# Fixing the order of TensorE's products and transposes in a mixture-of-experts stage

## The chip, the cores and the metric

One core of a Trainium2 chip runs the whole program. The metric is the device time of one launch in microseconds (us); several launches are timed and the median is told. One more launch is profiled, and its trace is what the rows below come from.

## What is computed

Two transformer layers over 256 tokens of width 1024, in float32. Layer 0 has stick-breaking attention and a dense SwiGLU. Layer 1 has softmax attention and a mixture of 8 experts, two of them per token. Only the experts matter here:

```python
def swiglu(h, w1, w3, w2):
    hid = silu(h @ w1) * (h @ w3)
    return hid @ w2
# w1, w3: 1024 x 3584, w2: 3584 x 1024, for each of 8 experts
y = sum(swiglu(t, e_w1[e], e_w3[e], e_w2[e]) * gate[:, e])
```

The weights of the experts are 8 x 3 x 3584 x 1024 floats, 352 MB, and each is read once.

## The kernel before, in words

**Products.** A float32 product is made of three faster ones (`mm3`, lines 175 to 179): each operand is split into a high part (`wh`) and a low part (`wl`), and high x high, high x low and low x high are added up in one PSUM bank. ScalarE (ACT in the rows) makes `wh` by a copy (line 154), VectorE (DVE) makes `wl` by a subtraction (line 155), which needs `wh`. Both work on 128x1024 pieces, and there are four buffers for each of `wh` and `wl`, so that a fifth piece can be split only when TensorE has done the products of the first.

**Loads.** SyncE (SP) loads the weights in pieces of 1 MB (two 128x1024 pieces each) into a ring of `raw` buffers, in the order in which they are used; a load is issued as soon as its buffer has been split.

**An expert** (lines 942 to 987) is seven chunks of 512 hidden columns. One chunk is:

- 24 products with its part of `w1` into one bank (four pieces; here called a1 to a4), then 24 with `w3` into another (b1 to b4). The stationary operand, the expert's tokens (`eh`, `el`), lies in `oh_t`.
- `gate_mul` (lines 585 to 593): ACT computes Silu of the first bank (line 587), DVE multiplies by the second (line 588) into `nat`.
- `hid_t` (lines 595 to 601), called one chunk later, between the `w1` and the `w3` products of the next chunk: four transposes on TensorE (PE, line 599) turn `nat`, into the bank that held the `w1` products. Then `split_out` (lines 181 to 183) splits the result into `hts`, two tiles in `ol_t`: ACT first (line 182), then DVE (line 183). `hts` exists once, so that this split has to wait for the last product that reads the chunk before it.
- `down` (lines 603 to 606), called one chunk later too, after `gate_mul`: 24 products of `hts` with four pieces of `w2` (d1 to d4), which add up over the expert's seven chunks in banks 0 and 1.

So the source's order on TensorE is: a1 to a4 of a chunk, the transposes of the chunk before, b1 to b4, d1 to d4 of the chunk before. At the end of an expert the tokens of the next are turned (`turn_x`, lines 871 to 878), and after its last `down` the sums leave through `yr` (`store_y`, lines 857 to 861: ACT line 859, DVE line 860). In the last expert four additions of rows stand on DVE as well (`add_rows`, lines 845 to 850), and the products of the last two chunks wait for them through `after=added` in `gate_mul`.

**What sets the order.** The source gives the order of the statements, but a planner (`schedule_with_timeline_sim=True`, line 1129) chooses each engine's real order: it plays the program through with its own idea of durations and lets an engine take, at each moment, the first instruction in source order that is ready. That order is then fixed, and each engine works through it strictly, waiting where something is not there yet. `behind((a, b))` (lines 106 to 113) forces `a` to come after `b` on their engine, without a semaphore. In the loop over the experts the kernel before uses it for `turn_x`, for `gate_mul` with `after` and in `stream`, and not for the products or for `hid_t`.

Of the kernel before, what the change touches and what calls it, by code (L numbers as in the profile page):

```python
# [17 lines left out]
P = 128  # L18
# [3 lines left out]
NC = D // P  # L22
# [5 lines left out]
FC = 512  # L28
# [17 lines left out]
def block_kernel(ctx: ExitStack, tc: tile.TileContext, x, w_qkv, w_o, mixer_norm, ffn_norm,  # L46
                 rel_bias, w1, w3, w2, router, e_w1, e_w3, e_w2, final_norm, onehot, out):
    nc = tc.nc
# [9 lines left out]
    bank = [psp.tile([P, FC], F32, name=f"bank{i}") for i in range(8)]  # L58
# [20 lines left out]
    ecs = [(f, min(FC, DFE - f)) for f in range(0, DFE, FC)]  # L79
# [26 lines left out]
    def behind(*pairs):  # L106

        for a, b in pairs:
            if b is not None:
                tc.add_manual_dep(a.ins, b.ins.name,  # L110
                                  mybir.DependencyInfo(mybir.DependencyClass.NoSync,
                                                       mybir.DependencyReason.DATA),
                                  reason="issue order")
# [24 lines left out]
    def stream(n, g=None, hold=(None, None), free=2):  # L138


        got = taken = 0
        while got < n:
            load_ahead()
            t = loaded[n_used[0]]
            _, nk, fn = jobs[n_used[0]]
            n_used[0] += 1
            k = min(nk, HALF // fn)
            for c0 in range(0, nk, k):
                wh = split.tile([P, HALF], F32R, name="wh")
                wl = split.tile([P, HALF], F32R, name="wl")  # L150
                m = k * fn
                src = t[:, c0 * fn:c0 * fn + m]
                if g is None:
                    i0 = nc.scalar.activation(wh[:, :m], src, AF.Copy)  # L154
                    i1 = nc.vector.tensor_sub(wl[:, :m], src, wh[:, :m].bitcast(F32))  # L155
                    if taken >= free:
                        behind((i0, hold[0]), (i1, hold[1]))
                else:
                    for c in range(k):
                        cs = slice(c * fn, (c + 1) * fn)  # L160
                        gc = gcol[:, g, got + c0 + c:got + c0 + c + 1]
                        i0 = nc.scalar.activation(wh[:, cs], src[:, cs], AF.Copy, scale=gc)  # L162
                        i1 = nc.vector.scalar_tensor_tensor(  # L163
                            wl[:, cs], src[:, cs], gc, wh[:, cs].bitcast(F32), op0=ALU.mult,
                            op1=ALU.subtract)
                        if taken >= free:
                            behind((i0, hold[0]), (i1, hold[1]))
                recent[0] = i0
                taken += 1
                for c in range(k):  # L170
                    yield wh[:, c * fn:(c + 1) * fn], wl[:, c * fn:(c + 1) * fn]
            got += nk
        assert got == n

    def mm3(ps, s, m, start, stop):
        i0 = nc.tensor.matmul(ps, s[0], m[0], start=start, stop=False)  # L176
        nc.tensor.matmul(ps, s[0], m[1], start=False, stop=False)  # L177
        i1 = nc.tensor.matmul(ps, s[1], m[0], start=False, stop=stop)  # L178
        return i0, i1

    def split_out(src, h, l):
        return (nc.scalar.activation(h, src, AF.Copy),
                nc.vector.tensor_sub(l, src, h.bitcast(F32)))  # L183
# [30 lines left out]
    ident = const.tile([P, P], F32, name="ident")  # L214
# [377 lines left out]
                                           op1=ALU.mult)  # L592
        return t

    def hid_t(t, n, ps, a, c, apart=True):
        k = n // P
        tv = t[:, :n].rearrange("p (f j) -> p j f" if apart else "p (j f) -> p j f", j=k)
        for j in range(k):
            nc.tensor.transpose(ps[:, j * P:(j + 1) * P], tv[:, j], ident)
        split_out(ps[:, :n], a[:, :n], c[:, :n])  # L600
        return [(a[:, j * P:(j + 1) * P], c[:, j * P:(j + 1) * P]) for j in range(k)]

    def down(ps, hT, j, w, start, stop):
        for half in range(2):
            mm3(ps[half], hT[j], tuple(a[:, half * FC:(half + 1) * FC] for a in w),
                start and j == 0, stop and j == len(hT) - 1)

    def dense_ffn(pool, hold, then):
        y = [[bank[0], bank[1]], [bank[2], bank[7]]]
# [172 lines left out]
    eh, el = (sp[0][:, i * D:(i + 1) * D].rearrange("p (c t) -> p c t", t=P) for i in range(2))  # L782
    hts = [sp[1][:, i * FC:(i + 1) * FC] for i in range(2)]
# [6 lines left out]
    tv = mp.tile([P, 2, NB], F32, name="tv")  # L790
# [80 lines left out]
    def turn_x(t, banks, later):  # L871

        for i in range(2):
            for c in range(4):
                cc = 4 * i + c
                behind((nc.tensor.transpose(bank[banks[i]][:, c * P:(c + 1) * P],
                                            t[:, cc * P:(cc + 1) * P], ident), later))
            take(i, banks[i])

    def gather(banks, later):  # L880


        def part(b, i, later):
            ps = bank[banks[i]]
            for c in range(4):
                cc = 4 * i + c
                i0 = nc.tensor.matmul(ps[:, c * P:(c + 1) * P], hn[b][:, cc * P:(cc + 1) * P],
                                      pe[:, b].bitcast(F32), start=b == 0 and c == 0,
                                      stop=b == NB - 1 and c == 3, skip_group_check=True)
                behind((i0, later))  # L890

        mark(0, 0)
        part(0, 0, later)
        later = numbers(1)
        part(0, 1, later)
        held[1] = mark(0, 1)
        for i in range(2):
            part(1, i, later)
            take(i, banks[i])
# [14 lines left out]
    y = [bank[0], bank[1]]  # L914
# [18 lines left out]
                i1 = nc.vector.tensor_add(ht[b][:, hs], ht[b][:, hs], ps)  # L933
        return i0, i1

    pend, done, added = None, None, None
    gather((3, 4), raws[2])
    k = 0
    most_v = None
# [2 lines left out]
    for e in range(NE):  # L942
        for i, (f0, n) in enumerate(ecs):
            b1, b3 = (5, 6) if k % 2 == 0 else (3, 4)
            k += 1
            for bk in (b1, b3):
                if bk == b3:
                    held[:] = None, None
                for c, w in enumerate(stream(NC, hold=held)):
                    _, last = mm3(bank[bk], (eh[:, c], el[:, c]), w, c == 0, c == NC - 1)  # L950
                if pend is not None and bk == b1:
                    hT = hid_t(pend[1], FC, bank[pend[2]], *hts)
            if i == len(ecs) - 1 and e + 1 < NE:
                turn_x(xr, (2, 7), last)
            t = gate_mul(ep.tile([P, FC], F32, name="nat"), bank[b1], bank[b3], n, after=added)
            if pend is not None:
                for j, w in enumerate(stream(4)):
                    down(y, hT, j, w, pend[0] == 0, pend[0] == len(ecs) - 1)
            pend = (i, t, b1)
            if i == 0:  # L960
                if e:
                    store_y(e - 1)
                else:
                    gates()
                    send()

                    cps = bank[2]
                    for b in range(NB):
                        nc.tensor.matmul(cps[:, :NE], ones, sel[:, b], start=b == 0,
                                         stop=b == NB - 1)  # L970
                    most = mp.tile([P, 1], F32, name="most")
                    nc.vector.tensor_reduce(most, cps[:, :NE], axis=mybir.AxisListType.X,
                                            op=ALU.max)
                    most_i = mp.tile([P, 1], mybir.dt.int32, name="most_i")
                    nc.vector.tensor_copy(most_i, most)
                    nc.vector.tensor_scalar(pos2, slot, -float(P), None, op0=ALU.add)
            if i == 1 and e + 1 < NE:
                xr = load_x(e + 1)
            if e == NE - 1:
                if i == 0:  # L980
                    for b in range(NB):
                        mark(e, b)
                    done = slots(e)
                elif i == 2:
                    came = [fetch(b) for b in range(NB)]
                elif i in (4, 5):
                    added = add_rows(i - 4, came[i - 4])
    hT = hid_t(pend[1], FC, bank[pend[2]], *(sp[0][:, i * FC:(i + 1) * FC] for i in range(2)))

    row = ep.tile([P, FC], F32, name="nat")  # L990
# [78 lines left out]
    for half in range(2):  # L1069
# [3 lines left out]
        i0, i1 = scatter(done, (half,), hts if half else ys)  # L1073
# [5 lines left out]
    for b in range(NB):  # L1079
# [3 lines left out]
        i1 = nc.vector.scalar_tensor_tensor(ms, ss[:, b, 1:2], 1.0 / D, ms, op0=ALU.mult,  # L1083
                                            op1=ALU.add)
# [49 lines left out]
```

## Time and profile before

| | |
|---|---|
| median of 3 launches | 1440.25 us (1438.56 to 1440.41) |
| profiled launch, its own time | 1438.46 us |
| its span, first to last instruction | 1436.8 us |
| TensorE | busy 1417.6 us (99%), 7285 matmuls and transposes |
| VectorE | busy 1170.2 us (81%) |
| ScalarE | busy 1010.3 us (70%) |
| mean granted TensorE clock | 0.996 of 2.4 GHz |
| DMA | 442.11 MB, mean 308 GB/s |

In the profile an instruction stands with the line that made it. A row of the timeline merges equal instructions in a row (x4 are four of them), and its first two numbers are the start of the first and the time from there to the end of the last. In brackets stands how long the engine was idle before, and whose result ended that. PEld is the load of the stationary operand of a product; it runs ahead of the products, so that a wait often shows there and not at PE. The ends of PE's instructions are modelled, so its starts are what is read here. The span's first 430 us or so are layer 0 and the attention of layer 1; the experts run from about 453 us to 1425 us.

### The profile page before, as it was taken

How to read it: one execution, taken by the hardware profiler on the slowest of the kernel's cores; microseconds unless marked ns; L12 is line 12 of the kernel's file. 1: busy time of each engine (PE TensorE's matmuls, PEld its weight loads, DVE VectorE, ACT ScalarE, POOL GpSimd, SP SyncE). 2: the span in 40 equal slices, each digit the busy share in tenths (PEclk: the TensorE clock that was granted, in tenths of full speed). 3: DMA queues.
4: the chain of work that ended last, by engine and by line, in shares of the span. 5: the costliest groups of instructions: out<-in, count | busy, mean ns of one | idle time of the engine just before them, and what ended most of it. 6: DMA issues, size and time to landing. Idle time of an engine off the chain costs nothing. (4 is left out here: it accounts for less than half of the span.)

```text
span 1436.8 us, 19637 instructions
## 1 busy us (share of the span) xinstructions
PE 1417.6 (99%) x7285; PEld 1176.7 (82%) x7285; DVE 1170.2 (81%) x1384; ACT 1010.3 (70%) x1282; POOL 45.3 (3%) x71
## 2 busy tenths in 40 slices
PE   9999999999999999999999999999999999999997
PEld 7877999988877888888888888878878887887775
DVE  6656766667667999999999988888888888898887
ACT  6656655546655778878878777777777777777765
POOL 1000000000001000000000000000000000000200
PEclk9999999999999999999999999999999999999998
DMA  9633865556566999999999999999999999999850
GB/s 353 236 117 108 303 196 186 186 173 228 180 246 218 402 401 388 385 373 373 388 392 362 391 362 373 366 381 368 354 389 372 357 380 380 358 374 369 320 189 32
DMA packets 172153, 442.11 MB, mean 308 GB/s; under 512 B 7299, under 2 KB 9395, under 8 KB 157972
## 3 DMA queue, kind: packets, MB, share of 16 engines
q1 hardware_dynamic: 166852, 422.61, 80.6%
q0 software_dynamic: 5136, 18.18, 3.5%
q8 instruction: 59, 0.97, 0.3%
q14 instruction: 42, 0.34, 0.1%
q10 hardware_dynamic: 64, 0.02, 0.0%
HBM read 430.00 MB, written 11.03 MB: 307 GB/s over the span
## 5 line engine op out<-in xcount | busy, mean ns | idle before, releaser
L155 DVE TENSOR_TENSOR wl<-raw,wh 128x1024 fp32r<-128x1024 f32 x710 | 834.4, 1220 | 112.9 <-ACT wh L154 106.0
L154 ACT ACTIVATE wh<-raw 128x1024 fp32r<-128x1024 f32 x710 | 725.6, 1057 | 133.9 <-PE bank L178 97.7
L177 PE MATMUL bank<-wl,oh_t 128*128 128x512 f32 x968 | 382.9, 396 | 2.9 <-DVE wl L155 2.0
L176 PE MATMUL bank<-wh,oh_t 128*128 128x512 f32 x968 | 375.5, 393 | 2.1 <-ACT wh L154 1.6
L178 PE MATMUL bank<-wh,oh_t 128*128 128x512 f32 x904 | 353.5, 391 | 0.1
L177 PEld LDWEIGHTS bank<-wl,oh_t 128*128 128x128 f32 x968 | 181.9, 188 | 60.0 <-DVE wl L155 18.9
L176 PEld LDWEIGHTS bank<-wh,oh_t 128*128 128x128 f32 x968 | 182.2, 188 | 41.4 <-ACT wh L154 1.8
L178 PEld LDWEIGHTS bank<-wh,oh_t 128*128 128x128 f32 x904 | 170.2, 188 | 34.1 <-DVE oh_t L183 0.8
L178 PE MATMUL bank<-wh,ol_t 128*128 128x512 f32 x504 | 194.6, 392 | 0.0
L162 ACT ACTIVATE wh<-raw,gcol 128x512 fp32r<-128x512 f32 (+1 forms) x192 | 123.8, 698 | 87.4 <-PE bank L318 56.3
L163 DVE SCALAR_TENSOR_TENSOR wl<-raw,gcol,wh 128x512 fp32r<-128x512 f32 (+1 forms) x192 | 131.1, 725 | 65.8 <-ACT wh L162 65.3
L177 PE MATMUL bank<-wl,ol_t 128*128 128x512 f32 x440 | 174.7, 397 | 0.4 <-DVE wl L155 0.4
L318 PE MATMUL bank<-x_h,wh 128*128 128x256 f32 x512 | 143.8, 282 | 0.0
L318 PE MATMUL bank<-x_h,wl 128*128 128x256 f32 x512 | 142.9, 280 | 0.0
L318 PE MATMUL bank<-x_l,wh 128*128 128x256 f32 x512 | 142.7, 279 | 0.0
L176 PE MATMUL bank<-wh,ol_t 128*128 128x512 f32 x440 | 137.1, 393 | 0.0
L178 PEld LDWEIGHTS bank<-wh,ol_t 128*128 128x128 f32 x504 | 94.4, 188 | 19.9 <-issue 1.1
L318 PEld LDWEIGHTS bank<-x_h,wh 128*128 128x128 f32 x512 | 95.9, 188 | 1.9 <-issue 1.1
L177 PEld LDWEIGHTS bank<-wl,ol_t 128*128 128x128 f32 x440 | 83.0, 189 | 16.4 <-DVE wl L155 0.6
L318 PEld LDWEIGHTS bank<-x_h,wl 128*128 128x128 f32 x512 | 96.1, 188 | 0.0
L318 PEld LDWEIGHTS bank<-x_l,wh 128*128 128x128 f32 x512 | 95.9, 187 | 0.2
L176 PEld LDWEIGHTS bank<-wh,ol_t 128*128 128x128 f32 x440 | 81.6, 188 | 16.8
(218 smaller groups left out, 1106.1 us busy)
## 6 DMA issues: line engine op xcount, KB each, us to landing
raw<-in_e_w_dram SPq DMA_DIRECT2D x335, 1024.0 KB, 7.3
raw<-in_w_dram SPq DMA_DIRECT2D x33, 1024.0 KB, 5.1
raw<-in_w_qkv_dram SPq DMA_DIRECT2D x22, 1024.0 KB, 5.7
raw<-in_w_o_dram SPq DMA_DIRECT2D x8, 1024.0 KB, 7.5
xs_d<-hn POOLq DMA_DIRECT2D x1, 4096.0 KB, 16.0
xr<-xs_d POOLq DMA_DIRECT2D x7, 512.0 KB, 7.5
ys_d<-yr POOLq DMA_DIRECT2D x7, 512.0 KB, 7.8
raw<-in_w_qkv_dram SPq DMA_DIRECT2D x4, 512.0 KB, 6.8
```

The source lines that it names most:

```text
L154: i0 = nc.scalar.activation(wh[:, :m], src, AF.Copy)
L155: i1 = nc.vector.tensor_sub(wl[:, :m], src, wh[:, :m].bitcast(F32))
L162: i0 = nc.scalar.activation(wh[:, cs], src[:, cs], AF.Copy, scale=gc)
L163: i1 = nc.vector.scalar_tensor_tensor(wl[:, cs], src[:, cs], gc, wh[:, cs].bitcast(F32), op0=ALU.mult, op1=ALU.subtract)
L176: i0 = nc.tensor.matmul(ps, s[0], m[0], start=start, stop=False)
L177: nc.tensor.matmul(ps, s[0], m[1], start=False, stop=False)
L178: i1 = nc.tensor.matmul(ps, s[1], m[0], start=False, stop=stop)
L318: nc.tensor.matmul(to, w[a][:, ms], z[:, :, c], start=c + i + m % 2 == 0, stop=c == NC - 1 and m % 2 == 1 and i == 2, skip_group_check=True)
```

## The change

`hid_t` and `down` get an argument `after`, and the loop over the experts carries `last`, the last product issued. Every group of three products of `w1` is put behind the last product of `down` before it, those of `w3` behind the last of `w1`, those of `down` behind the last of `w3`; the four transposes are chained behind the last product of `w1` and behind each other. Nothing else is changed: no instruction is added or removed, and no order is written for ScalarE, VectorE or the loads.

```diff
-    def hid_t(t, n, ps, a, c, apart=True):
+    def hid_t(t, n, ps, a, c, apart=True, after=None):
         k = n // P
         tv = t[:, :n].rearrange("p (f j) -> p j f" if apart else "p (j f) -> p j f", j=k)
         for j in range(k):
-            nc.tensor.transpose(ps[:, j * P:(j + 1) * P], tv[:, j], ident)
+            i0 = nc.tensor.transpose(ps[:, j * P:(j + 1) * P], tv[:, j], ident)
+            if after is not None:
+                behind((i0, after))
+                after = i0
         split_out(ps[:, :n], a[:, :n], c[:, :n])
         return [(a[:, j * P:(j + 1) * P], c[:, j * P:(j + 1) * P]) for j in range(k)]

-    def down(ps, hT, j, w, start, stop):
+    def down(ps, hT, j, w, start, stop, after=None):
         for half in range(2):
-            mm3(ps[half], hT[j], tuple(a[:, half * FC:(half + 1) * FC] for a in w),
-                start and j == 0, stop and j == len(hT) - 1)
+            i0, i1 = mm3(ps[half], hT[j], tuple(a[:, half * FC:(half + 1) * FC] for a in w),
+                         start and j == 0, stop and j == len(hT) - 1)
+            behind((i0, after))
+        return i1
...
-    pend, done, added = None, None, None
+    pend, done, added, last = None, None, None, None
...
                 for c, w in enumerate(stream(NC, hold=held)):
-                    _, last = mm3(bank[bk], (eh[:, c], el[:, c]), w, c == 0, c == NC - 1)
+                    i0, i1 = mm3(bank[bk], (eh[:, c], el[:, c]), w, c == 0, c == NC - 1)
+                    behind((i0, last))
+                last = i1
                 if pend is not None and bk == b1:
-                    hT = hid_t(pend[1], FC, bank[pend[2]], *hts)
+                    hT = hid_t(pend[1], FC, bank[pend[2]], *hts, after=last)
             if i == len(ecs) - 1 and e + 1 < NE:
                 turn_x(xr, (2, 7), last)
             t = gate_mul(ep.tile([P, FC], F32, name="nat"), bank[b1], bank[b3], n, after=added)
             if pend is not None:
                 for j, w in enumerate(stream(4)):
-                    down(y, hT, j, w, pend[0] == 0, pend[0] == len(ecs) - 1)
+                    i1 = down(y, hT, j, w, pend[0] == 0, pend[0] == len(ecs) - 1, last)
+                last = i1
```

## Rows read from the trace of the kernel before

**Rows 1.** Stretches by windows: length, busy time of each engine, clock, DMA share, GB/s.
```profile
480.18:598.96 118.78, 118.78 (x542) 98.81 (x541) 110.20 (x102) 96.01 (x102) 1.69 (x3) 1.00 1.03 393
598.96:717.72 118.76, 118.76 (x541) 98.80 (x540) 110.19 (x102) 95.99 (x102) 1.07 (x2) 1.00 1.01 380
835.90:957.50 121.60, 121.42 (x541) 97.80 (x540) 107.64 (x102) 92.01 (x102) 1.07 (x2) 1.00 1.01 372
...
1200.70:1304.82 104.12, 104.12 (x471) 84.73 (x470) 92.57 (x88) 79.38 (x89) 0.00 (x0) 1.00 1.01 369
1304.82:1375.84 71.02, 69.72 (x305) 55.33 (x304) 60.55 (x57) 52.36 (x58) 9.47 (x7) 1.00 0.95 348
1375.84:1395.81 19.97, 19.58 (x87) 15.54 (x85) 17.93 (x18) 11.67 (x13) 0.00 (x0) 1.00 0.34 121
1395.81:1416.52 20.71, 18.31 (x72) 14.36 (x73) 19.49 (x18) 15.63 (x17) 0.38 (x1) 0.92 0.00 1
```

**Rows 2.** Timeline, 717 to 735 us: a chunk of the first experts.
```profile
717.73 0.63 PE L599 MATMUL bank<-ident,nat 128*128 128x128 f32 x4
...
725.98 0.58 ACT L587 ACTIVATE nat<-bank 128x512 f32<-128x512 f32 x1
...
734.57 0.63 PE L599 MATMUL bank<-ident,nat 128*128 128x128 f32 x4
```

**Rows 3.** Waits of ACT, 480 to 800 us: total us, times, longest.
```profile
ACT ol_t L182 <- PE bank L177: 13.1, 17, 0.8
```

**Rows 4.** Waits of ACT, 818 to 1305 us.
```profile
ACT ol_t L182 <- PE bank L177: 43.9, 24, 2.0
ACT nat L587 <- PE bank L178: 36.1, 27, 1.5
```

**Rows 5.** Waits of PEld, 818 to 1305 us.
```profile
PEld bank L177 <- DVE wl L155: 13.7, 34, 0.6
```

**Rows 6.** Timeline, 835 to 848 us: a chunk of the later experts.
```profile
835.91 0.63 PE L599 MATMUL bank<-ident,nat 128*128 128x128 f32 x4
...
838.66 0.60 ACT L182 ACTIVATE ol_t<-bank 128x512 fp32r<-128x512 f32 x1 [1.95 <-PE bank L177]
...
844.15 0.39 PE L176 MATMUL bank<-wh,oh_t 128*128 128x512 f32 x1
...
844.35 0.60 ACT L587 ACTIVATE nat<-bank 128x512 f32<-128x512 f32 x1 [1.30 <-PE bank L178]
844.84 2.00 ACT L154 ACTIVATE wh<-raw 128x1024 fp32r<-128x1024 f32 x2
...
845.93 2.36 DVE L155 TENSOR_TENSOR wl<-raw,wh 128x1024 fp32r<-128x1024 f32 x2 [1.06 <-ACT wh L154]
...
846.87 0.39 PE L176 MATMUL bank<-wh,oh_t 128*128 128x512 f32 x1
847.21 0.50 PE L177 MATMUL bank<-wl,oh_t 128*128 128x512 f32 x1
847.55 0.40 PE L178 MATMUL bank<-wh,oh_t 128*128 128x512 f32 x1
```

**Rows 7.** Timeline, 468 to 470 us: the first expert's second chunk.
```profile
468.56 0.63 PE L599 MATMUL bank<-ident,nat 128*128 128x128 f32 x4
...
469.27 0.39 PE L177 MATMUL bank<-wl,oh_t 128*128 128x512 f32 x1
...
469.49 0.58 ACT L182 ACTIVATE ol_t<-bank 128x512 fp32r<-128x512 f32 x1
```

**Rows 8.** The last expert: line 847's durations, a wait of ACT, a window's clock.
```profile
L847 DVE SCALAR_TENSOR_TENSOR h<-raw,ex,h x4: 1275/1276/1279, 1391.6 to 1399.3; 128x1024 f32<-128x1024 f32 x4
...
1396.60 0.60 ACT L182 ACTIVATE ol_t<-bank 128x512 fp32r<-128x512 f32 x1 [5.52 <-PE bank L599]
...
1400.40:1403.80 3.40, 3.40 (x9) 2.32 (x8) 3.40 (x4) 1.64 (x2) 0.00 (x0) 0.55 0.00 0
```

**Rows 9.** Waits of SP, 818 to 1305 us.
```profile
SPq L130 <- DVE wl L155: 415.1, 169, 4.3
```

## The prediction

> **What bounds the kernel now.** TensorE is busy nearly all the time, so the first view is that of windows, cut from one set of transposes to the set seven chunks later, which is one expert's work [rows 1]. The first experts take 118.78 and 118.76 us with PE busy throughout; the later ones take 121.60 (three such stretches follow each other from 835.90; one is shown), then 104.12 for six chunks, 71.02 for four, and 19.97 and 20.71 for the last two. Same instructions, same clock, more time. A chunk of the first kind lasts 734.57 - 717.73 = 16.84 us [rows 2], and one expert's remainder, 118.78 - 7 x 16.84 = 0.90 us, is the turning of the next expert's tokens.
>
> Against this measure the later part loses 3 x 2.82 = 8.5 us in the three stretches, 104.12 - 6 x 16.84 - 0.90 = 2.2 in the fourth, 71.02 - 4 x 16.84 = 3.7 in the fifth and 40.68 - 2 x 16.84 = 7.0 in the last two [rows 1, 2]: 21.4 us in all. That is the most that an order of work can win here.
>
> The waits say how it is lost. From 818 to 1305 us the load of PE's stationary operand waits 34 times for a low part of weights, 13.7 us [rows 5]; before 800 us no such row stands in that view. DVE is late because ACT is. ACT's waits in that stretch are long in two places, up to 2.0 us at the split of the transposed chunk, which needs the last product on the old `hts`, and up to 1.5 us at Silu [rows 4]; before 800 us the first is at most 0.8 us [rows 3] and Silu starts without a wait [rows 2]. Neither costs anything by itself. But ACT works strictly in its order, so the pieces of weights behind the waiting instruction lose the lead of four buffers.
>
> One late chunk shows it step by step [rows 6]. The four transposes come at 835.91, in the middle of `down`. ACT's split of them stands next, and waits 1.95 us until `down` has let go of `hts`, at 838.66. Silu was put after b2, waits 1.30 us for the end of a4's products and starts at 844.35, 0.20 us after the next product begins (844.15). So b3 is split only at 844.84, its low part begins at 845.93, and the product that needs it starts at 847.21 instead of 846.87 + 0.23 = 847.10; after such a wait the next product also comes 0.34 us later, where 0.23 is usual. This one place costs 2 x 0.11 = 0.22 us per chunk, of 2.82 / 7 = 0.40 in all.
>
> **The change, part by part.** It adds and removes no instruction: matmuls, transposes, splits and DMAs are the same in number, and the order of products without a semaphore is free on PE. What it moves is four transposes, from inside `down` to the seam between a4 and b1.
>
> *The move on PE* costs nothing. The four transposes take the same place in the stream wherever they stand, and one instance of the new place is in the trace: in the first expert they stood inside a stretch of `w1` and `w3` products at 468.56; the second product after them started at 469.27 [rows 7], 0.71 later. That is 4 transposes and one product; without transposes it would be 0.23, so they cost 0.48 us, which the 16.84 us hold already. What waits next is ACT's split: there it started at 469.49 with no wait, and nothing was late.
>
> *The wait on `hts` goes.* `down` of the old chunk has ended 24 products earlier, so ACT's 1.95 us stall at 838.66 has no cause left. DVE's half follows ACT's and moves with it. The result is needed by d1 24 products later, 24 x 0.227 = 5.4 us, against 0.58 us on ACT [rows 7] and about as much on DVE: covered.
>
> *But the split now joins Silu.* Both become ready at the end of a4. Where ACT's order before was b1 b2 Silu b3, I expect b1 b2 Silu split b3, since nothing in the edit binds ACT, and the planner's order late in the run puts these instructions between loads that arrive in pairs of pieces (rows 6 show Silu between b2 and b3, and the pieces after it in one go of two). Counting from the first instruction after a4 (844.15 in rows 6, now the first transpose): Silu at +0.20; the split at +0.69, when the transposes (0.63 long [rows 2]) are just done; b3's split at +0.69 + 0.49 = +1.18; the low part's product 847.21 - 844.84 = 2.37 later, at +3.55. PE would want it at 847.10 - 844.15 = 2.95, plus 0.48 for the transposes, +3.43. It is late by 0.12, as it is now by 0.11: 0.22 us per chunk stay. Of the other 0.18 (the chunk in which `yr` leaves, which had three instructions in one place and now has one fewer, and the seam of experts) I take half away. So a late chunk loses 0.31 instead of 0.40.
>
> *Sum, against the profiled launch.* 27 chunks from 835.90 to 1304.82: 8.5 + 2.2 = 10.7 us lost before, 27 x 0.31 = 8.4 now: -2.3. The four after that: 3.7 before; 4 x 0.31 + 0.8 for a product with `w3` that still waits early on DVE, 2.0 now: -1.7. The last two: 7.0 before. Four additions of 1.28 us stand on DVE there, ACT's split waits 5.52 us behind them for the transposes, and the clock falls to 0.55 (the 1.2 GHz level for nearly all of the window) right after PE's gaps [rows 8]. The new place gives the transposes 24 products more before they hold up PE, but four additions of DVE work stay; bounds are 0 and 7 won, I take 3. Together -7.0: 1438.46 - 7.0 = 1431.5 for the profiled launch. The median of the launches shown is 1.8 us higher, 1440.25, which gives 1433.2; I say 1433.
>
> **Rivals.**
>
> *A. The good order holds to the end.* If the planner, now with PE's order given, places the split and Silu beside b3 and b4 as it did at 468.56 [rows 7], ACT waits for nothing and all late chunks take 16.84 us. 21.4 less some 3 for the additions: -18 to -19, 1421.5. For it: the new place has run without loss. Against: the late order begins while nothing in the source changes, and the edit removes no cause of that.
>
> *B. The split goes ahead of Silu on ACT.* In the source it stands first. Then it waits for the transposes (+0.68), Silu follows at +1.17, b3 at +1.66, its product at +4.03 against +3.43: late by 0.60, and with the 0.11 after it 0.71 per chunk instead of 0.31. That adds 31 x 0.40 = 12.4 us to the sum: 1445.6, slower. It decides where a late chunk loses more than 0.40 us. For it: source order wins where both are ready. Against: Silu is ready 0.4 us before the transposes are done.
>
> *C. The loads are the bound.* The later experts draw 372 GB/s, and if that were all there is, nothing would be won: 1440. Against it, the first experts drew 393 and 380 GB/s [rows 1], and SP sits waiting for free buffers, 415.1 us of 487 [rows 9]. The Trainium skill (DMA: Bandwidth & Descriptors, Where 436 GB/s comes from) says that for transfers between HBM and SBUF about 358 GB/s per core binds; by that limit no expert could get faster and the kernel would stay at 1440. The trace passes that figure in every expert window up to 1304.82 (and the same page tells of more for a core alone), so the chance is small.
>
> *D. It does not do what it says,* because the planner's order was the same in effect: no; the transposes at 835.91 stand inside `down`.
>
> **How the numbers follow.** About 0.2% (2.9 us) is what a measurement of this kernel can tell from no change. My forecast (b1 b2 Silu split b3, or neighbours of it such as b3 between the two) 0.55, with an own range of 1426 to 1440 from the bounds of the last two chunks (0 to 7) and of the half taken (0 to 0.18 per chunk); most of it, 0.46, is faster by over 2.9 us, the rest same. A 0.21: faster. B 0.18, slower, with 0.01 of it same; a worse place for DVE's product with `w3`, 0.03, slower. C 0.03: same. So faster 0.67, same 0.13, slower 0.20. The range reaches from A to just above B: 1420 to 1446.
>
> **What would show it.** Right: one set of transposes between the 24th and 25th product of every chunk; no row of ACT's split waiting for line 177; windows of seven chunks in the later part shorter than 121.60 and longer than 118.78; ACT's order there b1 b2 Silu split. Windows of 118.8 to the end would be A. B would show ACT's split waiting for line 599 with Silu behind it, and PEld waits for DVE above 13.7 us. The first experts staying at 118.8 would show that the move itself is free; if they grow, the step that costed it at nothing is wrong.

## The result and the profile after

The changed kernel takes 1447.87 us (median of 4 launches, 1446.96 to 1449.10) against 1439.40 us (1438.18 to 1440.41) for the kernel before on the same chip: the ratio is 1.0060, 95% interval 1.0048 to 1.0073. It is slower by 8.5 us; 1433 and "faster" were forecast, and the range ended at 1446. The profiled launch took 1449.10 us, its span is 1447.4.

The windows of the changed kernel, cut again from one set of transposes to another and with the columns of [rows 1]: two of the first experts, two of the later ones, the last chunk, what follows it up to the last transposes of the experts, the slow products inside the last chunk, and one long stretch, from the 22nd of the 56 sets of transposes to the last.

```profile
487.04:605.81 118.77, 118.77 (x541) 98.83 (x540) 111.45 (x102) 96.63 (x101) 1.69 (x3) 1.00 1.03 395
605.81:724.58 118.77, 118.77 (x541) 98.83 (x540) 111.44 (x102) 96.61 (x101) 1.07 (x2) 1.00 1.02 381
...
968.87:1092.57 123.70, 120.98 (x541) 98.27 (x540) 107.73 (x101) 94.35 (x101) 1.07 (x2) 1.00 0.99 366
1092.57:1216.27 123.70, 120.95 (x541) 98.27 (x540) 107.75 (x101) 94.38 (x101) 1.07 (x2) 1.00 0.99 367
...
1392.74:1416.19 23.45, 19.65 (x77) 15.34 (x76) 21.10 (x19) 14.37 (x15) 0.00 (x0) 0.87 0.01 4
1416.19:1427.04 10.85, 10.85 (x50) 9.09 (x49) 8.89 (x9) 8.67 (x10) 0.94 (x1) 0.96 0.01 2
1411.33:1415.60 4.27, 4.26 (x10) 3.39 (x11) 4.00 (x4) 1.06 (x1) 0.00 (x0) 0.50 0.00 0
...
827.14:1427.04 599.90, 583.89 (x2596) 473.80 (x2595) 522.71 (x489) 454.48 (x487) 14.78 (x14) 0.99 0.92 341
```

The first experts take 118.77 us, to a hundredth or two what they took [rows 1]. The later ones take 123.70 where they took 121.60: 4.93 / 7 = 0.70 us lost per chunk, against 0.40. The last chunk loses 23.45 - 16.84 = 6.6, and some 0.4 more go in the window behind it, at a clock of 0.96: 7.0, no less than was counted before. The long stretch takes 599.90; run 10 below does the same products in 570.56, without a wait. The kernel before needs for them, in a window cut to hold equally many:

```profile
825.89:1416.53 590.64, 585.85 (x2596) 471.17 (x2595) 522.21 (x489) 442.83 (x486) 13.05 (x14) 1.00 0.94 346
```

So 29.3 us are lost in this stretch, where 20.1 were lost before. The difference, 9.3, is most of the 10.6 us by which the two profiled spans differ; the medians differ by 8.5.

The waits of ACT and of PE's stationary operand, 818 to 1305 us (total us, times, longest):

```profile
ACT ol_t L182 <- PE bank L599: 57.1, 27, 2.1
...
PEld bank L177 <- DVE wl L155: 23.2, 29, 0.8
```

ACT's two long waits of before [rows 4] have become one: the split waits for the transposes. No row is left of Silu waiting, nor of the split waiting for line 177. But PE's operand now waits 23.2 us for the low parts instead of 13.7 [rows 5], with fewer and longer waits. One late chunk in the timeline, to be held beside [rows 6]:

```profile
1021.50 0.63 PE L599 MATMUL bank<-ident,nat 128*128 128x128 f32 x4
...
1022.17 0.60 ACT L182 ACTIVATE ol_t<-bank 128x512 fp32r<-128x512 f32 x1 [2.13 <-PE bank L599]
...
1022.66 0.59 ACT L587 ACTIVATE nat<-bank 128x512 f32<-128x512 f32 x1
...
1023.14 3.90 ACT L154 ACTIVATE wh<-raw 128x1024 fp32r<-128x1024 f32 x4
...
1024.23 2.36 DVE L155 TENSOR_TENSOR wl<-raw,wh 128x1024 fp32r<-128x1024 f32 x2 [0.74 <-ACT wh L154]
...
1024.74 0.39 PE L176 MATMUL bank<-wh,oh_t 128*128 128x512 f32 x1
...
1025.51 0.50 PE L177 MATMUL bank<-wl,oh_t 128*128 128x512 f32 x1 [0.39 <-DVE wl L155]
```

Counted from the transposes (1021.50): split +0.67, Silu +1.16, b3's split +1.64, the product with b3's low part +4.01, 0.77 after the product before it where 0.23 is usual. These are the numbers of rival B almost to the hundredth. Whether its reason (the split ahead of Silu) is also the right one is what the experiments ask.

The end, DVE and PE (the additions of rows are line 852 here):

```profile
1403.42 1.28 DVE L852 SCALAR_TENSOR_TENSOR h<-raw,ex,h 128x1024 f32<-128x1024 f32 x1
1404.62 1.22 DVE L155 TENSOR_TENSOR wl<-raw,wh 128x1024 fp32r<-128x1024 f32 x1
1405.75 1.28 DVE L852 SCALAR_TENSOR_TENSOR h<-raw,ex,h 128x1024 f32<-128x1024 f32 x1
1406.95 0.68 DVE L588 TENSOR_TENSOR nat<-nat,bank 128x512 f32<-128x512 f32 x1
1407.55 2.60 DVE L852 SCALAR_TENSOR_TENSOR h<-raw,ex,h 128x1024 f32<-128x1024 f32 x2
1410.06 4.62 DVE L155 TENSOR_TENSOR wl<-raw,wh 128x1024 fp32r<-128x1024 f32 x4
...
1411.34 0.79 PE L177 MATMUL bank<-wl,oh_t 128*128 128x512 f32 x1 [3.42 <-DVE wl L155]
1411.93 0.63 PE L178 MATMUL bank<-wh,oh_t 128*128 128x512 f32 x1
```

Between 1403.42 and 1410.06 DVE splits one piece. PE waits 3.42 us, and its next products start 0.43 us apart, at a granted clock of 0.50, the 1.2 GHz level.

### The profile page after: what moved, and what is told of

It is laid out like the page before. It is cut to its first block, busy times and chain, and to the rows that moved or that the text cites. A ratio compares the mean times of both kernels' runs of the same rounds, so it can differ in the third digit from the quotient of the medians.

```text
span 1447.4 us, 19564 instructions
## 1 busy us (share of the span) xinstructions
PE 1416.4 (98%) x7285; PEld 1179.9 (82%) x7285; DVE 1174.7 (81%) x1384; ACT 1023.6 (71%) x1282; POOL 47.7 (3%) x71
## 5 line engine op out<-in xcount | busy, mean ns | idle before, releaser
L154 ACT ACTIVATE wh<-raw 128x1024 fp32r<-128x1024 f32 x710 | 739.1, 1062 | 186.8 <-PE bank L178 147.5
L176 PE MATMUL bank<-wh,oh_t 128*128 128x512 f32 x968 | 383.6, 397 | 0.5 <-ACT oh_t L182 0.5
L178 PE MATMUL bank<-wh,oh_t 128*128 128x512 f32 x904 | 354.5, 392 | 0.4 <-DVE oh_t L183 0.3
L177 PE MATMUL bank<-wl,ol_t 128*128 128x512 f32 x440 | 171.5, 390 | 0.1
```

## The experiments

Eleven kernels ran, in three batches; each batch had its own runs of the kernel before, 1439.48, 1438.66 and 1439.61 us. The last column is a stretch of seven chunks with one turning of tokens from the later experts, by the view of windows; 118.8 is an expert without a wait.

| run | what is different | median us | ratio to before, 95% | seven chunks us |
|---|---|---|---|---|
| (changed kernel) | | 1447.87 | 1.0060 [1.0048, 1.0073] | 123.70 |
| 1 | only the transposes ordered | 1448.57 | 1.0059 [1.0041, 1.0077] | 123.66 |
| 2 | only the products ordered | 1435.28 | 0.9971 [0.9961, 0.9982] | 121.20 |
| 3 | Silu ahead of the split | 1448.91 | 1.0066 [1.0049, 1.0083] | 123.85 |
| 4 | two tiles for `nat` | 1442.49 | 1.0029 [1.0017, 1.0040] | 121.00 |
| 5 | control for 4 | 1456.89 | 1.0129 [1.0112, 1.0145] | 124.31 |
| 6 | Silu and split behind b4 | 1435.43 | 0.9973 [0.9963, 0.9984] | 121.21 |
| 7 | as 6, TensorE free | 1429.48 | 0.9937 [0.9920, 0.9954] | 120.66 |
| 8 | as 6, three more places mended | 1424.15 | 0.9903 [0.9887, 0.9920] | 118.80 |
| 9 | changed kernel, additions spread | 1444.80 | 1.0042 [1.0028, 1.0056] | |
| 10 | as 8, additions spread | 1420.95 | 0.9875 [0.9858, 0.9891] | 118.82 |
| 11 | as 10, TensorE free | 1420.36 | 0.9866 [0.9849, 0.9882] | 118.78 |

### Runs 1 and 2: the two halves of the change

Run 1 keeps the chain of the transposes and drops `behind` for the products:

```diff
                     i0, i1 = mm3(bank[bk], (eh[:, c], el[:, c]), w, c == 0, c == NC - 1)
-                    behind((i0, last))
                 last = i1
...
-                    i1 = down(y, hT, j, w, pend[0] == 0, pend[0] == len(ecs) - 1, last)
-                last = i1
+                    down(y, hT, j, w, pend[0] == 0, pend[0] == len(ecs) - 1)
```

> The other half of the change: the four transposes are chained behind the last product of w1, the products of w1, w3 and w2 are left free. The planned order of ACT is that of the changed kernel in the late chunks (b1 b2, split, Silu, b3). Theory 1: late chunks take about 17.5 us, seven of them 123.7, the whole 1447 (1444 to 1450). Theory 2: about that of the kernel before, 1438 to 1441.

Run 2 does the opposite:

```diff
-                    hT = hid_t(pend[1], FC, bank[pend[2]], *hts, after=last)
+                    hT = hid_t(pend[1], FC, bank[pend[2]], *hts)
```

> One half of the change: the products of w1, w3 and w2 are put in their order, the transposes are not chained. The planned order of ACT and DVE is that of the kernel before (split of the transposes between a2 and a3, Silu between b2 and b3). Theory 1: the late experts lose what they lost before, 121.6 us for seven chunks, the whole about 1440 (1436 to 1443). Theory 2 (PE's rigid order costs the time, and products are nearly all that PE does): 1446 to 1449.

Measured: 1448.57 us and 123.66 for seven chunks with the transposes alone; 1435.28 and 121.20 with the products alone. The whole loss comes with the four transposes. Written down alone, the order of the 72 products of a chunk loses nothing: it wins 4 us, 0.4 in each late expert and the rest near the end, and so ends 0.7 us under its range. The second theory, that TensorE's rigid order costs the time, falls for the late chunks.

### Run 3: Silu ahead of the split

This makes ACT's order the one the prediction had expected.

```diff
-                    hT = hid_t(pend[1], FC, bank[pend[2]], *hts, after=last)
+                    hT, parts = hid_t(pend[1], FC, bank[pend[2]], *hts, after=last, later=True)
...
             t = gate_mul(ep.tile([P, FC], F32, name="nat"), bank[b1], bank[b3], n, after=added)
+            if pend is not None:
+                behind((split_out(*parts)[0], silu[0]))
```

> The changed kernel, with ACT's order of the two instructions behind a4 turned round: Silu first, then the split of the transposes, b3 and b4 as before behind them. Theory 1 (ACT's fixed order costs the time, since b3 stands behind a split that waits 0.68 us for the transposes): the split starts at about +0.69 from the transposes, b3 at +1.18, the low product at about +3.55 where PE wants it at +3.43; a late chunk of the experts takes 17.1 to 17.2 us instead of 17.55, an expert of seven chunks 121.0 to 121.5 instead of 123.7, the whole about 1436 (1433 to 1440), 11 us under the changed kernel. Theory 2 (PE's rigid order itself costs the time, since PE can no longer take another product while one waits): nothing changes, 1446 to 1449.

Measured: 1448.91 us, 123.85 for seven chunks, no gain at all. This is 9 us above the range of theory 1, and that is the most useful result of the study. The number is the one that theory 2 named, but run 2 speaks against theory 2, so that a third cause was looked for. The timeline of a late chunk (Silu is line 589 here, the transposes 601):

```profile
1021.45 0.63 PE L601 MATMUL bank<-ident,nat 128*128 128x128 f32 x4
...
1022.11 0.60 ACT L589 ACTIVATE nat<-bank 128x512 f32<-128x512 f32 x1 [2.13 <-PE bank L601]
...
1022.61 0.59 ACT L182 ACTIVATE ol_t<-bank 128x512 fp32r<-128x512 f32 x1
...
1023.09 3.90 ACT L154 ACTIVATE wh<-raw 128x1024 fp32r<-128x1024 f32 x4
...
1025.46 0.50 PE L177 MATMUL bank<-wl,oh_t 128*128 128x512 f32 x1 [0.39 <-DVE wl L155]
```

Silu starts not at +0.20 but at +0.66, and what released it is the transposes. The waits of ACT between 830 and 1300 us, where the changed kernel has the split, now have Silu:

```profile
ACT nat L589 <- PE bank L601: 54.9, 26, 2.1
```

Silu does not read what the transposes write. But it writes `nat`, the transposes read the `nat` of the chunk before, and the pool `ep` (line 781 of the kernel before) is made with `bufs=1`, so that there is one `nat`. The new Silu may overwrite it only when the transposes are through. In the kernel before they stood in the middle of `down`, 8 us earlier [rows 6], and this bound nothing. The change puts them at the very place where Silu becomes ready.

### Runs 4 and 5: two tiles for `nat`, and the control

```diff
-RING1, RING2, RING3 = 1, 3, 3
+RING1, RING2, RING3 = 1, 2, 3
...
-            t = gate_mul(ep.tile([P, FC], F32, name="nat"), bank[b1], bank[b3], n, after=added)
+            t = gate_mul(ep.tile([P, FC], F32, name=f"nat{k % 2}"), bank[b1], bank[b3], n, after=added)
```

The second tile needs 2 KB of a partition, which one weight buffer less makes free. Run 5 has only that first line.

> The changed kernel with two tiles for nat, used by turns (and one weight buffer fewer in the last ring, to make room). Theory 1, mended after the run with Silu first: nat exists once in the changed kernel, the transposes read it, and Silu, which writes the next one, has to wait for them, so that Silu and the split both start 0.7 us late whichever stands first. With two tiles the planned order of ACT is b1 b2, Silu, split, b3, and Silu can start 0.2 us after the end of a4: b3's split then starts at +1.18 from the transposes instead of +1.64, its low product at +3.55 instead of +4.02; a late chunk takes 17.1 to 17.2 us instead of 17.55, an expert 121.0 to 121.5, the whole 1434 to 1442. Rival (Silu waits for something else after a4, or b3 is late for another reason): Silu starts at +0.66 as before, a late chunk takes 17.55, the whole 1446 to 1452.

> Control for the run with two nat: the changed kernel with one weight buffer fewer in the last ring, nat as it is. Loads land 7 us after their issue and are used some 41 us after it, so that a buffer less should cost nothing by itself; the planned order of ACT is the changed kernel's, only that the late order begins three chunks earlier. Both theories: late chunks 17.55 us, the whole 1447 to 1452 (three more late chunks are 2.1 us, the end may differ by 2). If it is under 1444, the buffer and not nat explains the run with two.

Measured: 1442.49 us with two tiles, 1456.89 with the buffer gone alone; seven chunks 121.00 and 124.31. A late chunk with two tiles:

```profile
1034.73 0.63 PE L599 MATMUL bank<-ident,nat 128*128 128x128 f32 x4
1034.93 0.60 ACT L587 ACTIVATE nat<-bank 128x512 f32<-128x512 f32 x1 [1.66 <-PE bank L178]
...
1035.43 0.59 ACT L182 ACTIVATE ol_t<-bank 128x512 fp32r<-128x512 f32 x1
...
1035.90 3.90 ACT L154 ACTIVATE wh<-raw 128x1024 fp32r<-128x1024 f32 x4
...
1038.28 0.50 PE L177 MATMUL bank<-wl,oh_t 128*128 128x512 f32 x1
```

Silu +0.20, split +0.70, b3 +1.17, its low product +3.55. No order was written for ACT here: with two tiles the planner put Silu first by itself, as it would if it takes what is ready first. So what the change added to the loss of the late chunks comes from the dependence on `nat`; turning the two instructions round without removing it gains nothing (run 3). The split first with two tiles was not run.

Two things did not go as written. The total of run 4 is 0.5 us over its range. The four additions stand two and two on DVE there, with only one other instruction between, and their chunk took 24.82 us; and from the last transposes to the end of the span it needs 24.7 us where the changed kernel needs 20.4. And the control is 5 us over its range: a buffer less is not free. Its long stretch takes 601.19, against 599.90, and it needs 25.5 us behind the last transposes, in part for this wait of TensorE for its own queue (the second row is the instruction at line 1071 that it waited for: count, then the least, median and greatest time in ns):

```profile
1437.09 0.47 PE L178 MATMUL bank<-wh,oh_t 128*128 128x512 f32 x1 [3.65 <-PEq L1071]
...
L1071 PEldq COMPARE_BRANCH  x1: 3699/3699/3699, 1433.2 to 1433.2; - x1
```

Line 1071 is a `tc.If` behind the experts, and its branch holds TensorE's queue for 3.70 us. The branch is no slower than in the changed kernel (3.74 us), but there twelve products still start while it runs and TensorE waits 1.0 us; in run 5 none does, and it waits for nearly all of it. Run 4 has such a wait too (4.1 us), so that it nearly cancels in their difference, 14.4 us. Of that the long stretch holds 601.19 - 587.89 = 13.3.

### Runs 6 and 7: nothing that waits ahead of a piece of `w3`

Run 6 leaves `nat` single and puts both waiting instructions behind b4. Run 7 is the same with the three `behind` of the change taken out again.

```diff
+            b4, b4l = recent[0], recent_l[0]
             t = gate_mul(ep.tile([P, FC], F32, name="nat"), bank[b1], bank[b3], n, after=added)
+            behind((silu[0], b4))
+            if pend is not None:
+                i0, i1 = split_out(*parts)
+                behind((i0, silu[0]), (i1, b4l))
```

> The changed kernel, with Silu put behind the split of b4 on ACT, the split of the transposes behind Silu, and its half on DVE behind the low part of b4: no instruction that waits for PE stands ahead of a piece of w3. PE's order is that of the changed kernel. Theory 1 (ACT's fixed order costs the time): the late chunks take 16.84 us like the early ones, except one chunk in seven in which the planner puts the multiplication into nat ahead of d1 on DVE (up to 1.9 us there); an expert 118.8 to 120.7 instead of 123.7, the whole 1420 to 1432. Theory 2 (PE's rigid order costs it): 1446 to 1449.

> The order of ACT and DVE of the run with Silu and the split after b4, but TensorE left free as in the kernel before (no product and no transpose is put behind another). Theory 1 (ACT's order decides, TensorE's order in itself neither costs nor gains): late chunks 16.84 us except where the multiplication stands ahead of d1, the whole within 3 us of that run's 1435.4, 1432 to 1439. Rival (TensorE's written order is needed for the gain): late chunks as in the kernel before, 1439 to 1444.

Measured: 1435.43 and 1429.48 us. In run 6 an ordinary late chunk takes 16.84 us, like the first ones, with one `nat` and the transposes at the seam:

```profile
1000.56:1017.40 16.84, 16.84 (x77) 14.00 (x76) 15.57 (x15) 13.61 (x14) 0.00 (x0) 1.00 1.01 363
```

The first experts of the changed kernel do the same by the planner's own choice. One of their chunks:

```profile
639.49 0.63 PE L599 MATMUL bank<-ident,nat 128*128 128x128 f32 x4
639.69 1.06 ACT L154 ACTIVATE wh<-raw 128x1024 fp32r<-128x1024 f32 x1 [0.30 <-PE bank L178]
640.66 0.58 ACT L182 ACTIVATE ol_t<-bank 128x512 fp32r<-128x512 f32 x1
641.13 0.59 ACT L587 ACTIVATE nat<-bank 128x512 f32<-128x512 f32 x1
```

There b4 is split at 639.69, before the two instructions, and neither waits. So in these kernels the dependence costs time only where they stand ahead of b3, as in the late chunks.

Run 6 as a whole is 3.4 us over its range, and seven chunks take 121.21 where 120.7 was the most expected. Part of what is left shows on DVE, in one chunk of seven where the multiplication into `nat` (line 590 here) stands ahead of d1 and waits for b4's products:

```profile
1352.39 0.69 DVE L590 TENSOR_TENSOR nat<-nat,bank 128x512 f32<-128x512 f32 x1 [3.04 <-PE bank L178]
```

That chunk loses 1.8 us, as expected of it; another 0.6 goes in the chunk in which `yr` leaves. Run 7 went below its range: with TensorE free the same orders of ACT and DVE give some 6 us more. So the order written for TensorE is not what wins here. A likely reason, which no run shows by itself, is that a fixed order leaves TensorE nothing else to take where another engine still stalls.

### Run 8: the three places that still lose

The multiplication goes behind d2's low part, `yr` behind a3's split, and the four additions are spread by hand.

```diff
+                if e and i == 1 and bk == b1:
+                    behind(*zip(store_y(e - 1), a3))
...
+                    if j == 1:
+                        i0 = nc.vector.tensor_mul(t[:, :n], t[:, :n], bank[b3][:, :n])
+                        behind((i0, recent_l[0]))
...
                 elif i in (4, 5):
-                    added = add_rows(i - 4, came[i - 4])
+                    add_row(0, i - 4, came[0], recent_l[0])
+                elif i == 6:
+                    for k2 in range(2):
+                        add_row(1, k2, came[1], recent_l[0])
```

> The run with Silu and the split after b4, with the three places mended that still lose time there: the multiplication into nat is put behind the low part of d2 on DVE (1.78 us in five chunks, 8.9), the output yr behind the split of a3 (0.6 in six chunks, 3.6), and the four additions of the last expert are spread, one after the fourth chunk's d4, one after the fifth's, two after the sixth's (3.7 us at the end, of which the half-speed products are 2). Theory 1: 16.84 us in every chunk up to the last two, an expert 119.0 instead of 121.2, the whole 1418 to 1423. Rival (DVE, with 15 to 16 us of work in 16.84, is now the bound and the time moves elsewhere): 1428 to 1435.

Measured: 1424.15 us, 118.80 for seven chunks, every chunk up to the last two without a wait. That it is 1 us over its range has its place: two of the additions came to lie behind the last chunk's pieces, and TensorE waited for a low part there.

### Runs 9 to 11: the additions

Run 9 is the changed kernel, runs 10 and 11 are run 8 (11 with TensorE free); in all three each addition stands between two given pieces on DVE, and the products of the last chunks no longer wait for the additions through `after=added`.

```diff
+                behind((i1, next_l[0]))
+                recent[0], recent_l[0], next_l[0] = i0, i1, None
...
+        behind((i0, recent_l[0]))
+        next_l[0] = i0
...
+                    if (e, i, bk, c) == (NE - 1, 6, b3, 3):
+                        add_row(1, 1)
...
+                if e == NE - 1 and (i, bk) in ((4, b3), (5, b1)):
+                    add_row(0, i - 4)
...
+                    if (e, i, j) == (NE - 1, 5, 1):
+                        add_row(1, 0)
```

> The changed kernel with nothing moved but the four additions of the last expert on DVE: one after the fifth chunk's b4, one after the sixth's a4, one after its d2, one after the last chunk's b2, and the next piece's low part put behind each. Theory: of the 6.6 us that the last chunk loses in the changed kernel, all but the usual 0.7 comes from the four additions standing in a row, and from the half clock that follows TensorE's gap; without them 5.9 us go, and 1.8 come back where the multiplication into nat has now got ahead of d1 in one chunk: 1442 to 1446, about 1443.8. The late chunks before stay at 17.55. Rival (the last pieces or the tail hold the end, whatever stands on DVE): 1446 to 1449.

> The run with three orders mended, with its four additions in the places of the other run of this batch (there two of them lay in the tail, where TensorE waited 2.3 us for a low part and went on at half clock, and one beside another, 1.0). Theory: no chunk over 16.84 to the end apart from the turning of tokens, no stretch at half clock in the last products, 4.3 us less: 1418 to 1421. Rival (the tail waits for something else): 1423 to 1425.

> The same with TensorE free (no product or transpose put behind another), so that only ACT's and DVE's orders are written down. Theory: where no engine stalls TensorE's order is worth nothing, within 2 us of the run beside it, 1418 to 1423. Rival (TensorE's written order costs, as the 6 us between the two runs with Silu and the split after b4 seem to say): 3 us or more less than the run beside it. Other rival (the written order is needed once the rest is in order): 3 us or more above it.

Measured: 1444.80, 1420.95 and 1420.36 us. Windows of run 9, the chunk before the last and the last:

```profile
1375.53:1397.64 22.11, 19.06 (x78) 15.04 (x76) 17.22 (x16) 14.39 (x15) 0.00 (x0) 0.92 0.82 308
1397.64:1414.48 16.84, 16.84 (x78) 14.00 (x76) 16.84 (x17) 13.62 (x14) 0.00 (x0) 1.00 0.01 2
```

The last chunk falls from 23.45 to 16.84: the additions, and the half clock after them, were its whole loss. The chunk before pays part of it back, 22.11 against 17.56, more than the 1.8 written down: an addition and the multiplication stand together there, and half clock follows again (0.92 on the mean). Windows of run 10, the long stretch and seven late chunks; there is no row of TensorE's operand waiting between 818 and 1305 us:

```profile
825.95:1396.51 570.56, 570.56 (x2595) 474.57 (x2594) 532.78 (x488) 461.56 (x486) 13.87 (x14) 1.00 0.96 359
927.91:1046.73 118.82, 118.82 (x542) 98.80 (x541) 110.45 (x102) 96.11 (x101) 1.06 (x2) 1.00 1.01 379
```

TensorE is busy in every part of it: 29.3 us less than the changed kernel in this stretch, and 20.1 less than the kernel before. Run 11, with TensorE free, is 0.6 us from it, well within what can be told apart. So the two rivals named for it fall: where nothing stalls, TensorE's written order is worth nothing and costs nothing that these runs can tell. Both are faster than the kernel before, by 1.25% and 1.34%.

## Why the prediction was wrong, step by step

**What bounds it: right, a little too large.** Run 10 wins by order alone the 20.1 us that the kernel before loses on the same products, and its median is 18.7 us under its runs of before. The 21.4 compare windows with whole chunks, and some windows hold a few products more: the last two hold 87 + 72 = 159 products and transposes [rows 1], two chunks 152, so that some 7 x 0.227 = 1.6 of their 7.0 us are work.

**The move on PE costs nothing: right.** 118.77 us against 118.78 and 118.76 [rows 1].

**The wait on `hts` goes: right.** No row of it is left.

**"But the split now joins Silu. Both become ready at the end of a4": this step failed.** It took Silu at +0.20 from [rows 6] and held that "nothing in the edit binds ACT". The edit binds it through `nat`, which the transposes read and Silu writes, and which exists once. Silu has to wait for the transposes in either order, so that b3's split starts at +1.64 where +1.18 was forecast, and a late chunk loses 0.70 us where 0.31 was. Run 3 shows it: with precisely the order that was forecast, b1 b2 Silu split b3, the product with b3's low part comes at +4.01, as in the changed kernel. Run 4 shows the working sound where the dependence is gone: +0.20, +0.70, +1.17 and +3.55 were measured where +0.20, +0.69, +1.18 and +3.55 were forecast. The loss there is (121.00 - 118.78) / 7 = 0.32 us per chunk, where 0.31 was forecast. The dependence could have been read ahead of time: the row of the transposes [rows 6] names `nat` as an input, the row of Silu names it as the output, and the first step of moving a reader is to ask who writes next. Before, Silu had waited for a4's products [rows 4], which hid it. The step explains most of the miss: 31 chunks x 0.39 = 12.1 us, and 3 more for the end as told below, make 1433.2 + 15.1 = 1448.3, against 1447.87.

**The planner's choice.** The forecast had Silu first because it would be ready 0.4 us earlier. Since both wait for the transposes, both are ready together, and the planner took the split, which stands first in the source. The rule by which rival B was argued, source order where both are ready, fits this; the evidence put against it was the failed step.

**The two last chunks: mis-sized.** 3 us of 7 were taken as won; none was. The additions stayed close together on DVE, TensorE waited 3.42 us and went on at half clock. Run 9 sizes it: with the additions spread the last chunk takes 16.84, so that its 6.6 us were theirs and the half clock's.

**The rivals.** B's price was right, 0.71 us per chunk against 0.70, and its total, 1445.6, is 2.3 us from the measured one; its mechanism was the trace's order but not its cause, as run 3 shows. Its chance of 0.18 was too small: with the dependence seen it was the case to forecast. A's time, 1421.5, is that of run 10, 1420.95, which needed ACT's and DVE's order written down and not TensorE's; that they agree so closely is partly luck, since A took 3 off for the additions, which run 10 has won too, from a sum that was too large. C, the loads as the bound, is out: run 10's late experts draw 379 GB/s, run 11's 381. The Trainium skill (DMA: Bandwidth & Descriptors, Where 436 GB/s comes from) has about 358 GB/s per core as what binds between HBM and SBUF; these windows, of the one core that runs here, pass it by 6%, so that the measurement decides. D is out: the transposes stand at the seam (1021.50, behind the last product of `w1`).

## What to carry to other kernels

Before an instruction is moved, ask of each tile that it reads how many copies there are and who writes it next: a wait that a trace has never shown can appear at the new place, and it falls on whoever stands behind the writer. In a kernel where a helper engine works in strict order, write down the helper's order (whatever waits goes behind the pieces that the bottleneck needs next) before that of the bottleneck; here the first, with DVE's, was worth 19.3 us (run 11) and the second, put on top, nothing that can be told (run 10). A price that is worked out right for a rival is a reason to look once more at the evidence that put the rival second.

## What the runs showed of the hardware

After TensorE had waited 3.42 us in the changed kernel, its granted clock was 0.50 for the next 4.27 us, with products 0.43 us apart instead of 0.23: ten products at 0.43 are some 2 us more, so that more than half of the wait was paid a second time. The branch of the `tc.If` behind the experts holds TensorE's queue for 3.3 to 4.1 us in every kernel of this study, where the other engines' take under 0.1; what it costs depends on the products that are already queued when it begins: 1.0 us of waiting in the changed kernel, 3.65 in run 5. With one weight buffer fewer (run 5) the span grew by 7.9 us, though its loads landed 7.1 us after their issue, as in the kernel before (7.3). The branch accounts for 2.7 of the 7.9; why the rest came with the buffer is open.
